# Making the low part of a weight split with an accumulating transfer in the down projection

## The chip, the cores and the metric

The kernel runs on one core of a Trainium2 chip. The metric is device time in microseconds (us) of one execution; lower is better. Before the change the median of three runs is 1138.18 us (1138.13 to 1138.3).

## The reference

One layer of a bidirectional encoder trunk over 1024 positions of width 1024, in float32: a combined input projection, three groups (convolution, recurrent, gating), an output projection, a gated feed-forward block, and a gate with an input embedding. The part that is changed belongs to the feed-forward block, whose inner width is 2816:

```python
h = rmsnorm(x, norm_ffn[l])
f = dwconv(h @ w_up[l], ffn_conv_w[l], ffn_conv_b[l], FFN_CONV_K // 2, FFN_CONV_K // 2)
fg, fu = jnp.split(f, 2, axis=-1)
x = x + (jax.nn.gelu(fg) * fu) @ w_down[l]
...
gate = jax.nn.sigmoid(rmsnorm(x, norm_ple[l]) @ w_ple_gate[l] + b_ple_gate[l])
```

## The kernel before, in words

TensorE multiplies in a reduced float32 format (fp32r). To keep accuracy, each operand is split into a high part, the value rounded to fp32r, and a low part, what the rounding lost. A product is then three matmuls that add into one accumulator: high by high, high by low, low by high (`mm3`). `split` makes the two parts: ScalarE copies the source into the high part with rounding, and VectorE subtracts the high part from the source to give the low part.

The down projection multiplies the gated activations g (2816 x 1024, kept transposed in DRAM as 22 tiles `g_dram[k]` of 128 x 1024) by w_down (22 row tiles of 128 x 1024). `prep_down` brings in one k: it loads `g_dram[k]` into a landing buffer (`raw`, three buffers that all such loads of the kernel share in turn), splits it, and calls `prep_rows`, which does the same for the row tile of w_down. Both loads are issued by SP. `down` runs one pass over up to four k: for each of the eight 128-row tiles of the output and each half of 512 columns, it adds 4 x 3 matmuls into an accumulator. The first pass (k = 0 to 3) is copied out by ScalarE; in later passes VectorE adds the accumulator to the running sum `x1` (tiles xA and xB). Passes 1 to 4 take k = 4 to 7, 8 to 11, 12 to 15 and 16 to 19; a last pass takes k = 20 and 21 and is joined with the gate. In pass 3 the residual rows are loaded and added too (`add_x1`).

A pass needs 16 buffers: high and low of g and of w for four k. There are two sets. Passes 0, 2 and 4 use the set `s1` (tiles L4, Y0, X3, L8, W0, L7, S0, W1 and the quarters of hT0 and hT1); passes 1 and 3 use `s2` (quarters of hT2, L0 to L3, quarters of hT3, G0 to G3). So in passes 1 and 3 the fourth tile of a pass stands in the tiles G, and in passes 2 and 4 the third and fourth stand in hT. A set can be filled again when the pass that used it has been multiplied, that is, while the other set is in use.

The order is not written by hand. Every operation is first recorded, and a planner (`Order`) then builds one order for all engines: it ranks the operations backwards from their users (`rank`, which puts a load 14 us, the constant FETCH, ahead of its user), places them one by one by estimated costs and landing times (`schedule`), plays that order through with shared transfers (`replay`), and keeps the best of six rounds by its own estimate (`plan`). The instructions are then issued in that order (line 461 issues them all, and so it is the line that every row of the profile names). Each engine takes its instructions in this fixed order and waits where an operand is not there. Transfers issued by GpSimd are in use for the constants at the start, the weights of the recurrent gates, eight stores of `e` and one load.

Of the kernel before, what the change touches and what calls it, by code (L numbers as in the profile page):

```python
# [10 lines left out]
F32 = mybir.dt.float32  # L11
F32R = mybir.dt.float32r
AF = mybir.ActivationFunctionType
ALU = mybir.AluOpType

P = 128
# [456 lines left out]
def encoder_layer(ctx, tc, x, p, norm_mix, w_in, conv_dw_w, conv_dw_b, conv_gn_g, conv_gn_b,  # L473
# [6 lines left out]
    V, A, PE, G, S = (Eng(od, e) for e in "VAPGS")  # L480
    x, p, out = x[0], p[0, 0], out[0]
    w_in, w_out, w_up, w_down = w_in[0], w_out[0], w_up[0], w_down[0]
# [20 lines left out]
    def raw(shape):  # L503
        return blk("raw", shape, bufs=3)
# [16 lines left out]
    def split(hi, lo, src, gain=None):  # L521
        if gain is None:
            A.activation(out=hi, in_=src, func=AF.Copy)
            V.tensor_tensor(out=lo, in0=src, in1=hi.bitcast(F32), op=ALU.subtract)
        else:
            A.activation(out=hi, in_=src, func=AF.Copy, scale=gain)
            V.scalar_tensor_tensor(out=lo, in0=src, scalar=gain, in1=hi.bitcast(F32),
                                   op0=ALU.mult, op1=ALU.subtract)
# [124 lines left out]
            r.append((hi, lo))  # L653
        return r

    def prep_rows(w, k, ring, gain=None):

        a = raw([P, T])
        S.dma_start(out=a, in_=w[k * P:(k + 1) * P, :])
        hi, lo = ring([P, T]), ring([P, T])  # L660
        split(hi, lo, a, gain)
        return hi, lo

    def mtile(wt, m, hT, ps=None, parts=((0, 512), (512, 512))):
# [87 lines left out]
    gl = [None] * 4  # L752
# [114 lines left out]
    e_dram = [od.tile(drp, [P, D], F32, f"e{t}", f"e{t}") for t in range(NT)]  # L867
    wple_r = Mixed("W4", "W5", "G2", "G3")
    wple = [prep_rows(w_ple, k, wple_r) for k in range(2)]
    ering = Ring(["L6", "L7", "L8"])  # L870
    rE = sm[:, 8:16]
# [162 lines left out]
    def w_out_rows(ring, *ks):  # L1034
        return [prep_rows(w_out, k, ring, cO[:, k:k + 1]) for k in ks]
# [194 lines left out]
    def set_of(*tags):  # L1230
        r = []
        for tag in tags:
            r += quarters(blk(tag, [P, 4, T], F32R)) if tag[0] == "h" else [tag]
        return r
# [3 lines left out]
    def prep_down(k, ring):  # L1238
        a = raw([P, T])
        S.dma_start(out=a, in_=g_dram[k])  # L1240
        gh, gl = ring([P, T]), ring([P, T])
        split(gh, gl, a)
        return (gh, gl), prep_rows(w_down, k, ring)

    def down(gw, after=None, first=False):
        n = len(gw)
# [22 lines left out]
    k = 0  # L1269
    sa = ["L4", "Y0", "X3", "L8", "W0", "L7", "S0", "W1"]  # L1270
    s1, s2 = sa + ["hT0", "hT1"], ["hT2"] + LS + ["hT3"] + GS
    for n, tags in enumerate((s1, s2, s1, s2, s1)):
        ring = Ring(set_of(*tags))
        down([prep_down(4 * n + j, ring) for j in range(4)], add_x1 if n == 3 else None, n == 0)
    k = 20
    ring = Ring(["L5", "L6"] + [f"W{j}" for j in range(2, 8)])
    last = [prep_down(k + j, ring) for j in range(2)]


# [3 lines left out]
    for k in range(8):  # L1283
        if k < 4:
            a = raw([P, T])
# [109 lines left out]
```

## Time and profile before

| | us |
|---|---|
| Median of three runs | 1138.18 |
| The profiled execution | 1138.66 |
| Its span, first to last instruction | 1136.9 |
| TensorE busy in the span | 1109.4 |
| VectorE busy | 820.5 |
| ScalarE busy | 558.5 |
| GpSimd busy | 25.5 |

The page gives the share of busy time of each engine and, in 40 slices, when it was busy. The table by stretch shows the same for chosen pieces of the span, with the granted TensorE clock and the load of the DMA engines. The timeline gives the instructions in order of start, with the idle time before one and what ended it. Pass 0 of the down projection begins at about 790 us among the last products of the up projection, pass 1 at about 836 us, pass 2 at about 880 us; one row tile of pass 3 runs from about 902 to 908 us, the rest from about 928 us; pass 4 begins at 967.5 us, and the gate follows.

### The profile page before, as it was taken

How to read it: one execution, taken by the hardware profiler on the slowest of the kernel's cores; microseconds unless marked ns; L12 is line 12 of the kernel's file. 1: busy time of each engine (PE TensorE's matmuls, PEld its weight loads, DVE VectorE, ACT ScalarE, POOL GpSimd, SP SyncE). 2: the span in 40 equal slices, each digit the busy share in tenths (PEclk: the TensorE clock that was granted, in tenths of full speed). 3: DMA queues.
4: the chain of work that ended last, by engine and by line, in shares of the span. 5: the costliest groups of instructions: out<-in, count | busy, mean ns of one | idle time of the engine just before them, and what ended most of it. 6: DMA issues, size and time to landing. Idle time of an engine off the chain costs nothing.

```text
span 1136.9 us, 13205 instructions
## 1 busy us (share of the span) xinstructions
PE 1109.4 (98%) x5305; PEld 929.8 (82%) x5305; DVE 820.5 (72%) x976; ACT 558.5 (49%) x720; POOL 25.5 (2%) x50
## 2 busy tenths in 40 slices
PE   6999999998999999999999999999999999999996
PEld 5987799887888888888888888888788888888885
DVE  6699999977966887687768776949433546654565
ACT  7555864779435475454545454536440222324445
POOL 3100100100000000000000000000000000000000
PEclk9999999999999999999999999999999999999999
DMA  8301240135032122232223222315640426421121
GB/s 296 99 1 56 94 162 20 53 101 185 22 122 96 39 74 93 75 111 74 69 80 112 74 74 75 111 56 192 235 147 2 148 85 212 130 75 40 72 74 55
DMA packets 55629, 110.60 MB, mean 97 GB/s; under 512 B 3977, under 2 KB 36594, under 8 KB 55568
## 3 DMA queue, kind: packets, MB, share of 16 engines
q1 hardware_dynamic: 53280, 104.35, 27.2%
q0 software_dynamic: 2288, 5.41, 1.3%
q8 instruction: 41, 0.67, 0.3%
q14 instruction: 20, 0.16, 0.0%
HBM read 85.63 MB, written 24.12 MB: 97 GB/s over the span
## 4 chain that ended last, share of the span: by engine, by line
PE 82%; DVE 13%; ACT 2%; issue 1%; DMA 1%; SPq 0%; DVEq 0%
PE pm L461 62%; PE pt L461 20%; DVE W L461 6%; DVE L L461 3%; DVE xA L461 1%; DMA xA<-in_x_dram 1%; DVE xB L461 1%; DVE G L461 1%; DVE hT L461 1%; ACT W L461 1%; ACT hT L461 0%; DMA raw<-in_w_down_dram 0%; ACT L L461 0%; ACT L461 0%; DVE V L461 0%
## 5 line engine op out<-in xcount | busy, mean ns | idle before, releaser
L461 PE MATMUL pm<-hT,W 128*128 128x512 f32 (+1 forms) x860 | 194.5, 369 | 0.1
L461 PEld LDWEIGHTS pm<-hT,W 128*128 128x128 f32 x860 | 149.8, 190 | 26.8 <-DVE hT L461 0.4
L461 PE MATMUL pm<-hT 128*128 128x512 f32 x480 | 124.6, 389 | 0.0
L461 PEld LDWEIGHTS pm<-hT 128*128 128x128 f32 x480 | 90.0, 188 | 19.2 <-DVE xA L461 0.4
L461 PE MATMUL pt<-hT,W 128*128 128x512 f32 x336 | 86.1, 389 | 0.0
L461 ACT ACTIVATE W<-raw 128x512 fp32r<-128x512 f32 (+1 forms) x60 | 44.9, 760 | 64.1 <-PE pt L461 47.8
L461 PEld LDWEIGHTS pt<-hT,W 128*128 128x128 f32 x336 | 63.1, 188 | 13.1
L461 DVE TENSOR_TENSOR xB<-xB,pm 128x512 f32<-128x512 f32 (+1 forms) x40 | 37.9, 950 | 42.5 <-PE pm L461 42.2
L461 PE MATMUL pm<-hT,hT 128*128 128x512 f32 (+1 forms) x256 | 66.2, 388 | 0.0
L461 ACT ACT_TABLE_LOAD x47 | 60.3, 1283 | 4.8 <-DVE W L461 2.4
L461 DVE TENSOR_TENSOR W<-raw,W 128x512 fp32r<-128x512 f32 (+1 forms) x57 | 47.1, 835 | 18.6 <-ACT W L461 18.6
L461 PEld LDWEIGHTS pm<-hT,hT 128*128 128x128 f32 x256 | 46.6, 188 | 8.9
L461 PE MATMUL pm<-L,L 128*128 128x512 f32 x160 | 50.3, 389 | 0.0
L461 DVE TENSOR_TENSOR xA<-xA,pm 128x1024 f32<-128x1024 f32 x20 | 24.4, 1219 | 35.1 <-PE pm L461 35.1
L461 DVE TENSOR_TENSOR X<-X,pm 128x512 f32<-128x512 f32 x20 | 13.7, 684 | 49.0 <-PE pm L461 49.0
L461 ACT ACTIVATE L<-raw 128x512 fp32r<-128x512 f32 (+1 forms) x19 | 15.8, 830 | 63.5 <-PE pm L461 35.0
L461 PE MATMUL pm<-xA,W 128*128 128x512 f32 x168 | 45.2, 389 | 0.0
L461 PE MATMUL pm<-W,hT 128*128 128x512 f32 x192 | 44.3, 390 | 0.0
L461 PE MATMUL pm<-L,hT 128*128 128x512 f32 (+1 forms) x160 | 43.7, 386 | 0.0
L461 ACT ACTIVATE hT<-raw 128x1024 fp32r<-128x1024 f32 x20 | 20.8, 1058 | 44.1 <-PE pm L461 31.4
L461 PEld LDWEIGHTS pm<-W,hT 128*128 128x128 f32 x192 | 35.9, 188 | 7.4
L461 PE MATMUL pt<-L,W 128*128 128x512 f32 x164 | 41.7, 390 | 0.0
(343 smaller groups left out, 2403.5 us busy)
## 6 DMA issues: line engine op xcount, KB each, us to landing
raw<-in_w_up_dram SPq DMA_DIRECT2D x44, 512.0 KB, 3.6
g<-xB SPq DMA_DIRECT2D x22, 512.0 KB, 2.7
raw<-g SPq DMA_DIRECT2D x22, 512.0 KB, 4.3
raw<-in_w_down_dram SPq DMA_DIRECT2D x22, 512.0 KB, 4.0
raw<-in_w_in_dram SPq DMA_DIRECT2D x16, 512.0 KB, 4.7
xA<-in_x_dram SPq DMA_DIRECT2D x8, 512.0 KB, 6.9
xB<-in_x_dram SPq DMA_DIRECT2D x8, 512.0 KB, 8.9
e<-L POOLq DMA_DIRECT2D x8, 512.0 KB, 3.2
```

The lines of the kernel that those rows point to most:

```text
L461: getattr(self.e[op.eng], meth)(*args, **kw)
```

## The change

`prep_rows` gets a flag `add`. With it, ScalarE writes the high part as before and then the negated high part into the low part's buffer; a transfer issued by GpSimd then reads the same rows of the weight from DRAM again and adds them to what stands in that buffer, which leaves weight minus high part. VectorE has no part in it. `prep_down` sets the flag for w_down tiles k = 4 to 19, that is, for passes 1 to 4; the split of g, and the tiles 0 to 3, 20 and 21 stay as they were.

```diff
-    def prep_rows(w, k, ring, gain=None):
+    def prep_rows(w, k, ring, gain=None, add=False):
 
         a = raw([P, T])
         S.dma_start(out=a, in_=w[k * P:(k + 1) * P, :])
         hi, lo = ring([P, T]), ring([P, T])
-        split(hi, lo, a, gain)
+        if add:
+
+            A.activation(out=hi, in_=a, func=AF.Copy)
+            A.activation(out=lo, in_=hi.bitcast(F32), func=AF.Copy, scale=-1.0)
+            G.dma_start(out=lo, in_=w[k * P:(k + 1) * P, :], accum_op=ALU.add)
+        else:
+            split(hi, lo, a, gain)
         return hi, lo
...
-        return (gh, gl), prep_rows(w_down, k, ring)
+        return (gh, gl), prep_rows(w_down, k, ring, add=4 <= k < 20)
```

## Rows read from the trace of the kernel before

**Rows 1.** The page's first two parts: busy time of each engine (share of the span, count of instructions), and the granted TensorE clock in 40 slices of 28.4 us, in tenths of full speed (9 is 90% or more).

```profile
PE 1109.4 (98%) x5305; PEld 929.8 (82%) x5305; DVE 820.5 (72%) x976; ACT 558.5 (49%) x720; POOL 25.5 (2%) x50
...
PEclk9999999999999999999999999999999999999999
```

**Rows 2.** Busy time by stretch: TensorE (count), its weight loads, VectorE, ScalarE, GpSimd, then granted clock, mean share of the DMA engines and GB/s.

```profile
0.00:50.00 50.00, 38.67 (x276) 36.78 (x276) 31.80 (x59) 30.49 (x52) 14.32 (x31) 1.00 0.64 214
...
100.00:200.00 100.00, 97.76 (x630) 88.21 (x629) 99.63 (x147) 63.37 (x83) 7.28 (x13) 1.00 0.24 84
200.00:300.00 100.00, 96.54 (x455) 79.77 (x453) 86.94 (x91) 75.52 (x80) 3.90 (x6) 0.98 0.29 96
...
780.00:810.00 30.00, 29.68 (x130) 24.16 (x131) 28.30 (x26) 20.38 (x21) 0.00 (x0) 1.00 0.78 261
810.00:833.00 23.00, 23.00 (x102) 18.64 (x102) 0.06 (x1) 4.11 (x4) 0.00 (x0) 1.00 0.30 123
833.00:849.00 16.00, 16.00 (x71) 12.90 (x70) 10.21 (x9) 10.09 (x10) 0.00 (x0) 1.00 0.62 200
849.00:881.00 32.00, 32.00 (x143) 26.40 (x142) 8.95 (x9) 2.35 (x3) 0.00 (x0) 1.00 0.10 32
881.00:897.00 16.00, 16.00 (x72) 13.28 (x71) 11.49 (x10) 5.93 (x6) 0.00 (x0) 1.00 0.69 234
897.00:930.00 33.00, 33.00 (x147) 27.32 (x147) 9.99 (x9) 2.62 (x3) 0.00 (x0) 1.00 0.09 30
930.00:952.00 22.00, 22.00 (x99) 18.23 (x98) 17.62 (x16) 7.78 (x8) 0.00 (x0) 1.00 0.79 263
952.00:1000.00 48.00, 48.00 (x214) 39.75 (x213) 28.65 (x24) 11.12 (x10) 0.00 (x0) 1.00 0.39 121
1000.00:1106.00 106.00, 106.00 (x497) 88.34 (x496) 59.22 (x60) 45.48 (x62) 0.00 (x0) 1.00 0.20 70
1106.00:1137.00 31.00, 21.60 (x122) 18.73 (x120) 16.95 (x31) 16.84 (x32) 0.00 (x0) 0.93 0.13 51
```

**Rows 3.** Waits of TensorE from 700 us to the end: who waited for whom, us in total, times, longest.

```profile
PE pm L461 <- ACT xA L461: 0.3, 1, 0.3
```

**Rows 4.** Timeline (start us, length us): the last splits of each pass's fill on VectorE and ScalarE, and the first matmuls on the tiles of passes 1 to 4.

```profile
808.83 1.23 DVE L461 TENSOR_TENSOR G<-raw,G 128x1024 fp32r<-128x1024 f32 x1 [0.78 <-ACT G L461]
...
840.70 0.84 PE L461 MATMUL pm<-G,G 128*128 128x512 f32 x3
...
848.23 1.23 DVE L461 TENSOR_TENSOR hT<-raw,hT 128x1024 fp32r<-128x1024 f32 x1 [0.86 <-ACT hT L461]
...
881.85 1.52 PE L461 MATMUL pm<-hT 128*128 128x512 f32 x6
...
892.74 1.06 ACT L461 ACTIVATE G<-raw 128x1024 fp32r<-128x1024 f32 x1 [1.47 <-DMA raw<-in_w_down_dram]
...
892.71 2.35 DVE L461 TENSOR_TENSOR G<-raw,G 128x1024 fp32r<-128x1024 f32 x2
...
903.61 0.84 PE L461 MATMUL pm<-hT 128*128 128x512 f32 x3
904.29 0.84 PE L461 MATMUL pm<-G,G 128*128 128x512 f32 x3
...
927.38 1.06 ACT L461 ACTIVATE L<-raw 128x1024 fp32r<-128x1024 f32 x1 [33.58 <-PE pm L461]
928.35 1.04 ACT L461 ACTIVATE X<-raw 128x1024 fp32r<-128x1024 f32 x1
...
940.97 2.22 ACT L461 ACTIVATE hT<-raw 128x1024 fp32r<-128x1024 f32 x2 [3.19 <-DMA raw<-g]
...
944.35 1.22 DVE L461 TENSOR_TENSOR hT<-raw,hT 128x1024 fp32r<-128x1024 f32 x1
...
968.89 1.52 PE L461 MATMUL pm<-hT 128*128 128x512 f32 x6
```

**Rows 5.** Timeline of ScalarE and TensorE at the one wait of the stage: a copy of a weight tile, the emptying of pass 0's first accumulator, and the matmul behind it.

```profile
807.74 1.06 ACT L461 ACTIVATE G<-raw 128x1024 fp32r<-128x1024 f32 x1 [0.69 <-DMA raw<-in_w_down_dram]
808.71 1.01 ACT L461 ACTIVATE xA<-pm 128x1024 f32<-128x1024 f32 x1
...
809.76 0.50 PE L461 MATMUL pm<-X,L 128*128 128x512 f32 x1 [0.32 <-ACT xA L461]
```

**Rows 6.** Groups of instructions of one shape, ScalarE from 833 to 1010 us and VectorE from 808 to 950 us: count, busy us, mean ns of one, idle time before them and who ended it.

```profile
L461 ACT ACTIVATE hT<-raw 128x1024 fp32r<-128x1024 f32 x12 | 12.6, 1062 | 39.9 <-PE pm L461 30.5 <-DMA raw<-g 6.7 <-DMA raw<-in_w_down_dram 2.6
...
L461 DVE TENSOR_TENSOR hT<-raw,hT 128x1024 fp32r<-128x1024 f32 x12 | 14.5, 1221 | 5.1 <-ACT hT L461 5.1
```

**Rows 7.** Transfers: GpSimd's only instruction after 250 us in the timeline (start, length, idle before), then issues by tile with the issuing queue, count, KB each and median us from issue to landing, and the least, median and longest landing of the loads of w_down.

```profile
270.99 0.59 POOL L461 DMA_DIRECT2D V<-in_norm_ffn_dram  x1 [56.26 <-PE pm L461]
...
raw<-in_w_down_dram SPq DMA_DIRECT2D x22, 512.0 KB, 4.0
...
e<-L POOLq DMA_DIRECT2D x8, 512.0 KB, 3.2
...
V<-in_norm_ffn_dram POOLq DMA_DIRECT2D x1, 512.0 KB, 5.7
...
DMA to landing us min/median/max: 3.3/4.0/8.3
```

**Rows 8.** Waits of SP's queue from 775 to 1010 us: us in total, times, longest.

```profile
SPq L461 <- DVE hT L461: 65.9, 22, 31.1
```

## The prediction

> **What bounds the kernel now.** I read the page first: TensorE is busy for 98% of the span, VectorE for 72%, ScalarE for 49%, and the granted clock is at its upper level in all 40 slices [rows 1]. A share of the whole span hides the stages, so the second view is the table by stretch [rows 2]. From 780 us to 1106 us, where the down projection and the start of the gate run, TensorE is idle only between 780 and 810 us, for 30.00 - 29.68 = 0.32 us; the later stretches show every microsecond as busy. Since a busy TensorE need not be a TensorE at its peak, I also looked at the spacing: three matmuls of 512 columns take 0.68 us from start to start (903.61, 904.29), 0.227 us each [rows 4] at clock 1.00. What is idle over the whole run, 1136.9 - 1109.4 = 27.5 us, lies elsewhere: 11.3 us in the first 50 us, 2.2 + 3.5 us between 100 and 300 us, 9.4 us in the tail after 1106 us [rows 2]. Third, the waits of TensorE after 700 us: one, for a ScalarE copy of an accumulated row, 0.3 us [rows 3]. So in the stage that is changed VectorE, ScalarE and the queues are all beside the path, and the question is only whether each tile is ready before the matmul that reads it.
>
> Each pass of the projection holds 8 x 2 x 4 x 3 = 192 matmuls, 192 x 0.227 = 43.6 us, and the 16 buffers of a pass are filled while the pass before it runs. The fourth reading is therefore, for each pass, the end of its last subtraction against the first matmul that needs that tile [rows 4]:
> - pass 1 (k = 4 to 7): 808.83 + 1.23 = 810.06 against 840.70, room of 30.6 us;
> - pass 2: 848.23 + 1.23 = 849.46 against about 882 (the two triples of matmuls on hT at 881.85), 32 us;
> - pass 3: 892.71 + 2.35 = 895.06 against 904.29, 9.2 us, since the planner puts the first row tile of pass 3 in the middle of pass 2;
> - pass 4: 944.35 + 1.22 = 945.57 against about 969 (968.89), 23 us.
>
> The tightest place, pass 3, decides the rival below.
>
> **The change, part by part.**
> Removed: 16 subtractions on VectorE of 1.22 us each [rows 6], 16 x 1.22 = 19.5 us. None is on the path: TensorE never waited for one after 700 us [rows 3]. Worth 0 to 0.32 us, the whole idle time of the stage; I take 0. Where the relief is largest, at 780 to 810 us (VectorE 28.30 of 30 us busy [rows 2]), TensorE's one wait was for ScalarE.
>
> Added on ScalarE: 16 negated copies. The same shape takes 1.06 us, and in a row they start 0.97 us apart (927.38, 928.35) [rows 4, 6], so 16 x 0.97 = 15.5 us. The copy waits only for the one before it on its own engine and for the buffer that the subtraction used to need, so nothing new blocks ScalarE's queue; what stands behind it is at most 0.97 us later. In passes 2 to 4 ScalarE has 8 to 10 us of work in a 16 to 22 us burst and under 3 us in the 32 us after it [rows 2], and the accumulated rows are taken off by VectorE there: cost 0. In 780 to 810 us it has 20.38 of 30 us, and it empties the accumulators too; there the four copies can stand in front of one of these. The shown case is 0.32 us, when the copy at 807.74 came before the emptying at 808.71 [rows 3, 5]. Bounds: 0 to 4 x 0.97 = 3.9 us; I take 0, nearest to that row, as the planner knows the copy's cost and ranks tiles of the next pass behind.
>
> Moved in time: the weights' landing buffer is now released by the copy and not by the subtraction after it, about 1.2 us earlier; SP's loads did wait for those subtractions, 65.9 us in 22 waits [rows 8]. The fill is not on the path, so this is 0 too, but it helps the new chain.
>
> Added on GpSimd's queue: 16 transfers of 512 KB that add in place. Issuing costs GpSimd about 0.59 us for a tile of this size [rows 7], and it had no instruction after 271 us; behind a waiting transfer stand only the transfers of later tiles. The trace shows no accumulating transfer, so its time A from issue to landing is bounded by neighbours [rows 7]: 3.2 us for a GpSimd-issued store of 512 KB below; above, twice the slowest load of w_down, 2 x 8.3 = 16.6 us, since the destination must be read as well. I take 5.7 us, the one GpSimd-issued load into such a tile, and one more passage of 0.524 MB at the 234 GB/s of 881 to 897 us [rows 2], 2.2 us: A = 7.9 us. It ends nearest to the 5.7 us row, which has engine, size and direction in common with it.
>
> The Trainium skill has a rule that speaks against the change (Collectives: The Full Stack, The bandwidth ceiling: the fold count and why AG ≠ RS ≠ AR): an addition in the DMA engines runs at half the rate of a copy, because two sources are read. No row here shows it. With the fixed 2.0 us and 436 GB/s that DMA: Bandwidth & Descriptors gives (Anatomy of one DMA), the plain transfer is 3.2 us, which the store's 3.2 us [rows 7] agrees with, and with doubled reading an estimate for A of 4.4 us; by the pages the sum would stay as it is.
>
> Engine capacity: the pass's eight loads keep the DMA engines 0.69 busy over 16 us [rows 2]; 234 / 0.69 = 339 GB/s is the full rate, 1.55 us for one passage. Eight loads and four additions of three passages are (8 + 12) x 1.55 = 31 us of a 43.6 us pass: it fits, and an addition's 4.6 us is about the 3 to 5 us between the weight copies of one pass, so they hardly pile up.
>
> The chain to the tightest tile: the copy of k = 15 ends at 892.74 + 1.06 = 893.80 [rows 4], the negated copy at 894.8, the addition at 894.8 + 7.9 = 902.7. The first use is at 904.29: in time by 1.6 us, if the order of TensorE stays. In pass 4 the last copy ends at 940.97 + 2.22 = 943.19, so A may reach 968.89 - 944.2 = 24 us there, and more in passes 1 and 2. So nothing reaches the path, and the sum is 0.
>
> Sum: the profiled execution took 1138.66 us, 1136.9 us of it span; 1138.66 + 0 = 1138.7, and the median of the runs is 0.48 us below that execution: **1138.2 us**.
>
> **The rivals.**
> *The addition comes late in pass 3 (slower).* TensorE's order is fixed when the kernel is built, so when one operand is late it stands. If the early row tile of pass 3 keeps its place, the stall is A - 9.5 us (904.29 - 894.8): it decides from A = 9.5 us on, is measurable from 11.8 us, and at A = 16.6 us costs 7.1 us: 1145.3 us. For it: the room of 9.2 us, no measured price, additions and loads at the same time. Against it: the planner charges the transfer with a landing time of its own before it places that row tile, and all other passes have much room. Should A exceed 24 us, more passes would be late and the time past 1150 us; nothing in the rows is that slow.
>
> *ScalarE in front of the emptying (slower).* The four copies at 780 to 810 us delay accumulators: up to 3.9 us, 1142 us. For it: the 0.3 us wait is of just this kind. Against it: 9.6 us of ScalarE are free in that stretch.
>
> *The order of everything is redrawn.* The planner builds the order from all operations at once, ranks each backwards from its users, and keeps the best of six rounds. The additions rank the weight loads about 13 us earlier than before (FETCH 14 and a copy in place of a subtraction), and another round may win. That can change the idle time outside the stage, 17 us in the first 300 us and 9.4 us in the tail, either way. A tenth of these 26.4 us gone would be 1138.2 - 2.7 = 1135.5 us; as much lost, 1140.9 us. For it: that idle time is real. Against it: the work of the first 700 us and of the tail is unchanged, and nothing in the change touches what those waits are for.
>
> *The change does nothing because the subtractions were hidden anyway*: this is the forecast itself.
>
> **How the numbers follow.** A measurement of this kernel tells about 0.2% from no change, 2.3 us: 1135.9 to 1140.5. Forecast, within that: 0.61. Late additions: 0.17. ScalarE in front: 0.06. Redrawn order: 0.12 faster, 0.04 slower. So faster 0.12, same 0.61, slower 0.27. The forecast's own range, with 0.32 us less and the small part of a stall, is 1137 to 1140. The range reaches down to 1135.5 (redrawn) and up to 1146 (A at its upper bound); I leave out about 0.16: larger redraws below, and additions slower than any row above.
>
> **What would show it.** Right: TensorE busy without a gap from 810 to 1106 us as in [rows 2]; 19.5 us less on VectorE and about 15.5 us more on ScalarE; additions landing in 5 to 10 us; in every pass the landing before the first matmul of its tile. The late rival: a wait of TensorE or of its weight load for the addition, at the first matmuls on G and L of a pass. ScalarE in front: waits for xA or xB at 800 to 815 us. Redrawn: the first 300 us or the tail with other idle time, and stage boundaries shifted already ahead of 760 us. I would be wrong if an addition took over 11.8 us, or if the new order left less room than the old.

## The result and the profile after

The changed kernel takes 1146.65 us, median of five runs (1144.17 to 1150.18), against 1138.18 us (1137.95 to 1139.7); the ratio is 1.0074, 95% interval 1.0055 to 1.0092. It is slower by more than the 0.2% that can be told, and 0.65 us above the stated range. The profiled execution after is the fastest of the five, 1144.17 us with a span of 1142.4 us; what the median has above it, 2.5 us, stands in no trace.

First the page and the table by stretch of the changed kernel, in the columns of [rows 1, 2]:

```profile
PE 1107.0 (97%) x5305; PEld 927.8 (81%) x5305; DVE 802.8 (70%) x961; ACT 567.9 (50%) x732; POOL 39.1 (3%) x66
```

```profile
0.00:50.00 50.00, 32.72 (x244) 31.43 (x245) 33.80 (x70) 30.28 (x54) 14.36 (x31) 1.00 0.61 204
50.00:100.00 50.00, 49.27 (x225) 40.32 (x224) 43.34 (x63) 39.15 (x37) 2.85 (x5) 1.00 0.11 35
100.00:200.00 100.00, 96.82 (x591) 85.95 (x590) 99.90 (x148) 45.61 (x63) 4.32 (x8) 1.00 0.24 82
...
810.00:833.00 23.00, 23.00 (x102) 18.82 (x102) 2.45 (x2) 9.90 (x10) 1.73 (x2) 1.00 0.94 289
...
897.00:930.00 33.00, 32.17 (x142) 26.32 (x141) 8.47 (x7) 2.64 (x3) 1.74 (x2) 1.00 0.44 124
...
1106.00:1142.00 36.00, 27.11 (x147) 23.30 (x145) 19.88 (x33) 17.89 (x33) 0.00 (x0) 0.93 0.15 59
```

Read the column of TensorE against [rows 2]. The first 50 us have 32.72 us of work where there were 38.67: most of the loss is 750 us ahead of the changed code. The stage that was changed has lost only 0.83 us, in 897 to 930 us. The work moved roughly as planned: VectorE 820.5 - 802.8 = 17.7 us less, ScalarE 9.4 us more (16 copies more, but three table loads fewer, among others), GpSimd 13.6 us more.

The waits of TensorE say who was late (us in total, times, longest); the first two lines are of the first 320 us, the other two of 780 us to the end:

```profile
PE pt L461 <- DVE L L461: 11.5, 3, 7.9
PE pt L461 <- DVE hT L461: 7.0, 3, 6.0
...
PE pm L461 <- DMA G<-in_w_down_dram: 0.8, 1, 0.8
PE pm L461 <- DVE hT L461: 0.4, 1, 0.4
```

The early ones are waits for the normalised rows and their transposes at the very start of the kernel. The same two in the kernel before, in the same window:

```profile
PE pt L461 <- DVE L L461: 8.6, 3, 8.0
PE pt L461 <- DVE hT L461: 3.2, 1, 3.2
```

All waits of TensorE in these 320 us together are 16.7 us before and 24.4 us after. Of the four lines of the changed kernel, only the third is the change at work: the addition into G, the fourth tile of pass 3, the place that the prediction named. Here are the issue of this addition and the matmul that waited, in the timeline:

```profile
898.90 0.87 POOL L461 DMA_DIRECT2D G<-in_w_down_dram  x1 [0.97 <-ACT G L461]
...
909.07 0.73 PE L461 MATMUL pm<-G,G 128*128 128x512 f32 x2 [0.83 <-DMA G<-in_w_down_dram]
```

And the view of the DMA queues: GpSimd's queue (packets, MB, share of 16 engines' span), then the additions by tile as in [rows 7]:

```profile
q0 software_dynamic: 4592, 13.80, 5.3%
...
hT<-in_w_down_dram POOLq DMA_DIRECT2D x8, 512.0 KB, 8.5
L<-in_w_down_dram POOLq DMA_DIRECT2D x4, 512.0 KB, 7.9
G<-in_w_down_dram POOLq DMA_DIRECT2D x2, 512.0 KB, 7.8
W<-in_w_down_dram POOLq DMA_DIRECT2D x2, 512.0 KB, 8.1
```

These are medians by tile, 7.8 to 8.5 us from issue to landing; the estimate was 7.9 us. The single additions took 5.4 to 10.8 us, and the one that TensorE waits for, issued at 898.90 us, took 10.1 us.

The kernel's own planner explains why the start changed. It keeps the best of six rounds by its estimate; before, the first round was the best, with the change the fourth. The two programs do the same work at the start of the kernel, but the fourth round puts it in another order than the first.

### The profile page after: what moved, and what is told of

Same layout as the page of the kernel before. It is cut to its first block, busy times and chain, and to the rows that moved or that the text cites. A ratio compares the mean times of both kernels' runs of the same rounds, so it can differ in the third digit from the quotient of the medians.

```text
span 1142.4 us, 13234 instructions
## 1 busy us (share of the span) xinstructions
PE 1107.0 (97%) x5305; PEld 927.8 (81%) x5305; DVE 802.8 (70%) x961; ACT 567.9 (50%) x732; POOL 39.1 (3%) x66
## 5 line engine op out<-in xcount | busy, mean ns | idle before, releaser
L461 DVE TENSOR_TENSOR X<-X,pm 128x512 f32<-128x512 f32 x20 | 13.7, 683 | 67.0 <-PE pm L461 67.0
L461 ACT ACTIVATE xB<-xB 128x1024 f32<-128x1024 f32 x22 | 23.3, 1061 | 40.0 <-DVE xB L461 40.0
```

The source lines that it names most:

```text
L461: getattr(self.e[op.eng], meth)(*args, **kw)
```

## The experiments

Theory R: the loss is the redrawn order, above all the other round. Theory D: it is the additions themselves, late or in the way. A third, L, came out of the first runs. The runs were made in three rows (1 to 3, 4 to 7, 8 and 9); in each the kernel before ran on the same chip beside them, with a median of 1137.83, 1138.15 and 1138.27 us.

**1. The change, held to the planner's first round.** In `plan`, on the changed kernel:

```diff
-            if best is None or span < best[0]:
+            if n == 0:
```

> The change in full, but the planner is held to the order of its first round, the round that the kernel before was issued in; up to the output projection's second half (about 340 us) the order is then the kernel before's. Theory R (the loss comes from the redrawn order: with the change, the planner's own estimates make another of its six rounds win, and the new order has more idle TensorE time in the first 300 us): TensorE busy 38 to 39 us in the first 50 us, as before, and 1138 to 1140 us, what is left over 1138.2 being a late addition of about 1 us. Theory D (the additions and copies themselves cost the time, by late operands and contention in the down projection): 1144 to 1147 us, as the changed kernel.

Measured: 1149.08 us (1148.4 to 1149.93), ratio 1.0098 (1.0085 to 1.0112). The start is as before (38.88 us of TensorE in 50 us), and yet it is the slowest of all. R alone had failed. Timeline of ScalarE and TensorE in this run:

```profile
816.53 1.06 ACT L461 ACTIVATE G<-raw 128x1024 fp32r<-128x1024 f32 x1 [5.29 <-DMA raw<-in_w_down_dram]
817.62 1.06 ACT L461 ACTIVATE G<-G 128x1024 fp32r<-128x1024 f32 x1
818.58 1.01 ACT L461 ACTIVATE xA<-pm 128x1024 f32<-128x1024 f32 x1
...
819.64 0.70 PE L461 MATMUL pm<-X,L 128*128 128x512 f32 x1 [4.48 <-ACT xA L461]
820.13 0.63 PE L461 MATMUL pm<-L,L 128*128 128x512 f32 x1
820.56 0.63 PE L461 MATMUL pm<-X,Y 128*128 128x512 f32 x1
```

And the landing of all transfers from w_down, additions included, in the view of that tensor (least, median, longest), then the table by stretch:

```profile
DMA to landing us min/median/max: 3.4/7.6/13.9
...
810.00:833.00 23.00, 18.52 (x75) 14.73 (x74) 1.23 (x1) 6.57 (x7) 0.87 (x1) 0.93 0.70 206
```

ScalarE stands 5.29 us for the plain load of k = 7, which took 13.9 us from issue at 802.56 to landing; the slowest before took 8.3 us [rows 7]. Behind that copy, in ScalarE's fixed order, stand its negated copy (817.62) and the emptying of an accumulator, and TensorE waits 4.48 us for the latter. Then its matmuls start 0.43 us apart, not 0.227 us, for some 3 us: the granted clock of 810 to 833 us is 0.93 here, so part of that stretch ran at the lower level. Two more waits follow, 2.5 us for an emptied accumulator and 0.8 us for an addition. The 2.5 us stand behind a load too, on VectorE: its additions into xA come after a split that waits 10.68 us for ScalarE's copy of a g tile, which waits for loads. From 780 to 1006 us TensorE stands 226 - 218.24 = 7.8 us and starts 945 matmuls, where the kernel before stands 0.3 us and starts 992; 47 x 0.227 = 10.7 us, so of the loss about 3 us are matmuls at the lower clock. Theory L: an addition keeps the DMA engines so long that the plain loads beside it come late, and what stands behind these loads in the fixed orders comes late with them.

**2. The kernel before, held to the planner's fourth round.** The same edit with `if n == 3:` on the kernel before; no additions.

> The kernel before, without any addition, held to the order of the planner's fourth round, the one that the changed kernel was issued in; up to about 350 us the order is then the changed kernel's. Theory R: 1143 to 1147 us and TensorE busy near 33 us in the first 50 us, with the wide spread of the changed kernel's runs, though no addition is there. Theory D: 1138 us, as before.

Measured: 1145.48 us (1144.03 to 1145.62), ratio 1.0064 (1.005 to 1.0077). The table by stretch:

```profile
0.00:50.00 50.00, 32.57 (x243) 31.28 (x244) 33.64 (x70) 30.32 (x54) 14.35 (x31) 1.00 0.60 204
```

The waits of TensorE in the first 320 us:

```profile
PE pt L461 <- DVE L L461: 11.6, 3, 8.0
PE pt L461 <- DVE hT L461: 7.1, 3, 6.0
```

These are the waits of the changed kernel, without one addition. So the other round costs 1145.48 - 1137.83 = 7.6 us, as R expected. The wide spread did not come with it.

**3. The changed kernel, transfers that overwrite.** `accum_op=ALU.add` is taken out of the transfer; the order is the changed kernel's. The low part is then the weight itself, so the kernel leaves out the subtraction of the high part and its result is not the layer's.

> The changed kernel in its own order, instruction for instruction, but the 16 transfers of GpSimd overwrite and do not add, so that the low part of these weight tiles is the weight itself. Theory R: 1145 to 1147 us still; only the 0.8 us wait for the late addition goes, and the plain transfer lands in 4 to 6 us against 7.6 us. Theory D: 1139 to 1142 us, since the reading of the destination is gone.

Measured: 1145.57 us (1143.13 to 1145.81), ratio 1.0062 (1.0049 to 1.0075), as R expected: in the issued order of the changed kernel, adding costs about 1 us at most, and that is not clear of noise (1.0074, 1.0055 to 1.0092, with the adding). The landing is a little over the 4 to 6 us expected. The view of the DMA queues, to be set beside that of after:

```profile
q0 software_dynamic: 4592, 13.80, 3.5%
...
hT<-in_w_down_dram POOLq DMA_DIRECT2D x8, 512.0 KB, 6.9
L<-in_w_down_dram POOLq DMA_DIRECT2D x4, 512.0 KB, 5.6
G<-in_w_down_dram POOLq DMA_DIRECT2D x2, 512.0 KB, 6.0
W<-in_w_down_dram POOLq DMA_DIRECT2D x2, 512.0 KB, 5.5
```

Before, this queue took 1.3% of 1136.9 us on the page, 14.8 us of all 16 engines. Less that, 16 plain transfers took 0.035 x 1143.8 - 14.8 = 25.2 us, 1.58 us each, and 16 additions 0.053 x 1142.4 - 14.8 = 45.8 us, 2.86 us each: 1.8 times as long, for the same bytes counted. (The shares are rounded to 0.1%, so each sum is good to some 0.6 us.)

**4. Experiment 1, transfers that overwrite.** The edits of 1 and 3 together.

> The change held to the planner's first round, as in the run with 1149 us, instruction for instruction, but the 16 transfers overwrite and do not add, so that the low part of these tiles is the weight itself. That run's loss has one long wait for an accumulator (4.5 us) behind a load of w_down that took 13.9 us, and two shorter ones. Theory L (an addition keeps the DMA engines longer than a plain transfer, and the plain loads beside it come late): the waits shrink to under 1 us each, the slowest load of w_down is back near 8 to 10 us, and the time is 1138 to 1141 us. Theory B (it is the additional 8 MB in themselves, added or not): about 1146 to 1149 us.

Measured: 1137.7 us (1136.14 to 1138.89), ratio 0.9995 (0.9985 to 1.0005). All 11 us of experiment 1 are gone with the adding alone, at the same order and the same number of transfers: theory L, and not the 8 MB more in themselves. The waits of TensorE after 700 us in this run:

```profile
PE pm L461 <- DVE xA L461: 0.7, 1, 0.7
PE pm L461 <- ACT xA L461: 0.3, 1, 0.3
```

The landing of its transfers from w_down:

```profile
DMA to landing us min/median/max: 3.4/5.7/10.1
```

The slowest is the load of k = 7 again, issued at 802.77 us: 10.1 us here, 13.9 us in run 1, 5.4 us in the kernel before. So the further plain transfers, or the order that differs from before, delay it too; the 3.8 us that adding puts on top are what the order has no room for.

**5. The kernel before in its own order, with additions.** At issue, the place of each subtraction is taken by two instructions:

```diff
+        split(hi, lo, a, gain)
         if add:
...
+            od.swap[od.ops[-1]] = [
+                ("A", "activation", (), dict(out=lo, in_=hi.bitcast(F32), func=AF.Copy, scale=-1.0)),
+                ("G", "dma_start", (), dict(out=lo, in_=w[k * P:(k + 1) * P, :], accum_op=ALU.add))]
...
-            for meth, args, kw in op.calls:
+            for e, meth, args, kw in self.swap.get(op, [(op.eng, *c) for c in op.calls]):
```

> The kernel before in its own order to the last matmul; only at the place of each of the 16 subtractions stand the negated copy on ScalarE and the addition on GpSimd. This is the sum of the prediction, with the planner taken out of it. The prediction's theory (each addition lands ahead of its matmuls): 1138 to 1139 us, no wait over 0.5 us from 780 to 1000 us. Rival, late addition in pass 3: one wait of 0 to 2 us at the first G of pass 3 near 904 us, 1138 to 1141 us. Theory L (additions make the plain loads late, and ScalarE, which waits for such a load, has the emptying of an accumulator behind it): a wait of TensorE for ScalarE's xA or xB between 805 and 820 us of 3 to 6 us, and 1141 to 1146 us.

Measured: 1143.9 us (1141.66 to 1146.81), ratio 1.0057 (1.0038 to 1.0077). This is the sum of the prediction, and it is 5.7 us off. The time is in theory L's range; its one wait of 3 to 6 us came as two of 1.4 and 1.5 us, and the late addition came beside it. Timeline of TensorE (its four waits from 780 to 1000 us), then of ScalarE at three of them, and of ScalarE and GpSimd for the tightest tile:

```profile
808.59 0.50 PE L461 MATMUL pm<-X,L 128*128 128x512 f32 x1 [1.50 <-ACT xB L461]
812.28 0.50 PE L461 MATMUL pm<-X,L 128*128 128x512 f32 x1 [1.36 <-ACT xA L461]
840.55 0.96 PE L461 MATMUL pm<-hT 128*128 128x512 f32 x3 [0.60 <-ACT xB L461]
909.80 0.73 PE L461 MATMUL pm<-G,G 128*128 128x512 f32 x2 [2.04 <-DMA G<-in_w_down_dram]
...
804.36 1.06 ACT L461 ACTIVATE hT<-raw 128x1024 fp32r<-128x1024 f32 x1 [2.37 <-DMA raw<-in_w_down_dram]
...
806.59 1.04 ACT L461 ACTIVATE hT<-hT 128x1024 fp32r<-128x1024 f32 x1
807.53 1.00 ACT L461 ACTIVATE xB<-pm 128x1024 f32<-128x1024 f32 x1
810.26 1.06 ACT L461 ACTIVATE G<-raw 128x1024 fp32r<-128x1024 f32 x1 [1.72 <-DMA raw<-in_w_down_dram]
811.23 1.01 ACT L461 ACTIVATE xA<-pm 128x1024 f32<-128x1024 f32 x1
...
838.55 1.04 ACT L461 ACTIVATE L<-X 128x1024 fp32r<-128x1024 f32 x1
839.50 1.00 ACT L461 ACTIVATE xB<-pm 128x1024 f32<-128x1024 f32 x1
...
894.15 1.06 ACT L461 ACTIVATE hT<-raw 128x1024 fp32r<-128x1024 f32 x1 [3.09 <-DMA raw<-in_w_down_dram]
899.53 1.06 ACT L461 ACTIVATE G<-raw 128x1024 fp32r<-128x1024 f32 x1 [1.36 <-DMA raw<-in_w_down_dram]
...
901.98 0.88 POOL L461 DMA_DIRECT2D G<-in_w_down_dram  x1 [4.32 <-ACT G L461]
```

1.50 + 1.36 + 0.60 + 2.04 = 5.5 us, nearly the whole loss. Both rivals of the prediction are here at their places. Of ScalarE's share, the 1.36 us stand behind a late load (810.26), the 0.60 us behind a negated copy (838.55), and the 1.50 us behind one of each (804.36, 806.59). The load of 810.26 is that of k = 7: it was issued at 802.33 us, as before (802.34), and took 7.9 us where it took 5.4. The addition for k = 15 was reckoned to be issued at 894.8 us and was issued at 901.98: the copies for k = 14 and 15 start at 894.15 and 899.53, where the last one started at 892.74 [rows 4]. Of these 7.2 us, 3.5 us are no loss of room, since the three waits ahead of it shift the first use as well, from 904.29 to 909.80 - 2.04 = 907.76. The other 3.7 us leave 5.8 us of room for a landing that took 7.8 us. They come from the loads: that of k = 14 took 8.2 us (4.5 before), and that of k = 15 was issued at 895.24 (889.19 before), after a wait of SP for the copy of k = 14. This order was not run with overwriting transfers, so how its loss divides between the adding and the further transfers is not shown here.

**6. Experiment 1 without pass 1's additions.** `add=8 <= k < 20`, first round.

> First round of the planner, and only the tiles k = 8 to 19 with the addition; those of pass 1 are split as before. Theory L: pass 1's tiles are filled beside the last loads of the stage before, where the DMA engines are busiest and ScalarE empties accumulators; without the additions there, the wait of 4.5 us near 815 us and the slower clock behind it go, some 6 us: 1140 to 1143 us, with the waits near 860 and 905 us still there. If the loss had another place: 1147 us or more.

Measured: 1144.68 us (1144.14 to 1145.19), ratio 1.0063 (1.0048 to 1.0078). Half a hit: from 780 to 897 us TensorE is now busy throughout, which fits a stall near 815 us that comes from pass 1's additions. It does not prove it, since the planner, given other ranks, drew the order anew. The only wait of TensorE after 700 us is that for G in pass 3, 2.3 us. But the time is above the forecast, with time lost elsewhere in the new order (the waits, then the table by stretch, same columns):

```profile
PE pm L461 <- DMA G<-in_w_down_dram: 2.3, 1, 2.3
...
300.00:400.00 100.00, 96.77 (x452) 79.99 (x451) 70.97 (x74) 41.54 (x76) 0.00 (x0) 0.97 0.23 79
```

**7. Experiment 1, with the planner told what an addition costs.** Three times the bytes and 3.0 for 0.9 us of landing, in `schedule` (and the bytes in `replay`):

```diff
+                nb *= 3 if "accum_op" in op.calls[0][2] else 1
...
-                end = dma + 0.9 if op.land is None else max(dma + 0.9, t + op.land)
+                end = dma + (3.0 if "accum_op" in op.calls[0][2] else 0.9) if op.land is None else max(dma + 0.9, t + op.land)
```

> The change in full in the planner's first round, but the planner is told that an addition moves three times its bytes and lands 2.1 us later than it assumed. Theory L: if the stalls are an order built on too short a landing time, the planner now puts the accumulators' emptying and the early matmuls elsewhere, and the time falls from 1149 us to 1138 to 1143 us. If it stays at 1147 us or more, the engines' time for additions is the limit, whatever the order.

Measured: 1136.61 us (1135.19 to 1137.63), ratio 0.9986 (0.9977 to 0.9995), better than forecast. All 16 additions are there; the stalls are not. The waits of TensorE after 700 us:

```profile
PE pm L463 <- ACT xA L463: 0.4, 1, 0.4
```

The slowest plain load still took 13.7 us. So the engines can carry the additions, and late loads need not cost anything; it was the order that could not carry them. With these costs the planner also takes the first round by its own choice, and the issued order is this one.

**8. and 9. That order with subtractions, and experiment 7 again.** In 8, at issue, the negated copy's place is taken by VectorE's subtraction and the transfer is left out:

```diff
+            od.swap[od.ops[-1]] = [("V", "tensor_tensor", (),
+                                    dict(out=lo, in0=a, in1=hi.bitcast(F32), op=ALU.subtract))]
             G.dma_start(out=lo, in_=w[k * P:(k + 1) * P, :], accum_op=ALU.add)
+            od.swap[od.ops[-1]] = []
```

> The order of the run with 1136.6 us (first round, planner told what an addition costs), instruction for instruction, but at the place of each negated copy VectorE subtracts as before, and the 16 transfers of GpSimd are left out. If what that run has over the kernel before comes from its order: 1136 to 1137 us again. If it comes from the work taken off VectorE and the landing buffers freed earlier: 1138 us or more.

> The run with 1136.6 us once more, beside the one above on the same chip, to tell the two apart: 1136 to 1137.5 us, 0.05 to 0.25% under the kernel before.

Measured: 1136.48 us (ratio 0.9983, 0.9974 to 0.9992) with subtractions, 1136.41 us (0.9982, 0.9974 to 0.9991) with additions. The 0.2% over the kernel before are the order's; between adding and subtracting there is nothing to be told. Table by stretch of run 9, then of run 8:

```profile
780.00:810.00 30.00, 30.00 (x134) 24.75 (x133) 22.05 (x21) 23.52 (x24) 2.67 (x3) 1.00 0.84 262
...
881.00:897.00 16.00, 16.00 (x72) 13.25 (x71) 7.29 (x7) 8.27 (x8) 3.37 (x4) 1.00 1.00 275
```

```profile
780.00:810.00 30.00, 30.00 (x133) 24.34 (x132) 26.72 (x25) 20.49 (x21) 0.00 (x0) 1.00 0.77 252
...
881.00:897.00 16.00, 16.00 (x72) 13.28 (x71) 12.15 (x11) 5.32 (x5) 0.00 (x0) 1.00 0.72 223
```

TensorE is full in both; VectorE has 12.15 us of work in 16 with subtractions and 7.29 us with additions, and it makes no difference.

## Why the prediction was wrong

**What bounds the kernel** was right, and with it that the subtractions are worth nothing: runs 8 and 9 differ by 0.07 us. In the order of these two the sum of 0 holds.

**The step that failed most: the redrawn order.** It was a rival, with a price of 2.7 us either way and a chance of 0.04 for slower, on the argument that "the work of the first 700 us and of the tail is unchanged". The work is unchanged, but the order is chosen as a whole, and another of the six rounds has another start. The price was a tenth of the idle time, taken without a reason for that share. Run 2 gives the price, 7.6 us, and the waits at the start show its place. This is most of the measured 8.5 us (1146.65 - 1138.18).

**The second: "the sum is 0".** In the order of before the additions cost 5.7 us (run 5), in the re-ranked first round 11.3 us (run 1: 1149.08 - 1137.83), in the order that was issued about 1 us at most (run 3 against the result). The duration A was right as a median, 7.9 us estimated, 7.8 to 8.5 measured; at the tightest place of the changed kernel it was 10.1 us. What failed above all is the start of the chain: the landing of the plain loads was carried over from [rows 4] as if the additions did not touch it. The capacity sum (31 of 43.6 us) even had an addition too dear, 4.6 us of the engines for the 2.86 of run 3. But it is an average over a pass, and loads and additions come in one burst: [rows 2] showed 0.62 to 0.79 busy there before anything was added, and it is up to 0.94 after. Three landing buffers then hand a late load on to the next, as for k = 14 and 15 in run 5.

The Trainium skill's rule that an addition in the DMA engines runs at half the rate of a copy (Collectives: The Full Stack, The bandwidth ceiling: the fold count and why AG ≠ RS ≠ AR) is stated there for the add of a ring collective, which no run here has; run 3 beside after comes near it, 2.86 against 1.58 us of the engines, 1.8 times. The prediction's estimate of 4.4 us for the landing, by the 2.0 us and 436 GB/s of the Trainium skill (DMA: Bandwidth & Descriptors, Anatomy of one DMA), was too short: the quickest addition took 5.4 us. The 3.2 us that the same figures give for a plain transfer agreed with the store of [rows 7], but not with the load of 5.7 us beside it.

**"Nothing new blocks ScalarE's queue"** was wrong in its scope. The negated copy indeed adds no wait beyond its own length, but the copy of the high part ahead of it waits for a load, and that load was now late; in runs 1 and 5 the accumulators stood behind it. The rival ScalarE in front of the emptying had the right place (808 to 820 us) and the smaller half of the cause: run 5 shows 0.60 us and a part of 1.50 us from the copies themselves, the rest from waiting for a transfer. Of run 1's 4.48 us, the negated copy between load and emptying (817.62 to 818.58) is 0.96 us and the late load the rest.

**Late addition in pass 3**: right in place, 0.83 us in the changed kernel, 2.04 us in run 5. In the changed kernel the mechanism is the rival's too: the room from issue to first use was 909.07 - 0.83 - 898.90 = 9.3 us, and the landing took 10.1. In run 5 the landing was as estimated, 7.8 us, and the room had shrunk to 5.8 us by the late loads.

**The tail** kept its idle time, 36.00 - 27.11 = 8.9 us to 1142 us, 9.4 us before [rows 2]. **Open**: the spread of the changed kernel's five runs, 6 us, which neither run 2 (1.6 us) nor run 3 (2.7 us) showed and run 5 did (5.2 us); in runs 7 and 9, which add without a stall, it is 2.4 us. Open is also why run 8's order is 0.2% better than that of before. A part can be seen, 0.5 us less idle between 300 and 400 us and 0.3 us at 780 to 810 us; the rest was not followed up.

## What to carry to other kernels

Where an automatic planner orders the whole program, test a local edit with the order held, as in runs 2, 5 and 8: otherwise the draw of the order (7.6 us here) can hide what the edit does. Where a transfer becomes heavier, ask which loads share its burst and what stands behind the engine that waits for those loads; its own landing time is the smaller part of the question. And when an operation of a new kind enters a planned order, give the planner its cost: that alone turned 1149 us into 1136.6 us, though the cost given was only near the measured one (three times the bytes, where 1.8 times the engines' time was measured).

## What the runs showed of the hardware

An adding transfer of 512 KB took 2.86 us of all 16 DMA engines, an overwriting one of the same shape 1.58 us. It landed in 7.8 to 8.5 us against 5.5 to 6.9 us (medians by tile; single ones 5.4 to 10.8 us against 4.1 to 8.6 us), and GpSimd was busy 0.87 us with its issue, 0.54 us without the adding. The slowest plain load of w_down took 8.3 us before, 10.1 us (run 4) and 11.9 us (run 3) beside overwriting transfers, and 13.9 us (run 1) and 16.5 us (run 5) beside additions. After a stall of TensorE of 4.5 us its matmuls started 0.43 us apart for some 3 us, where 0.227 us is the rule, with a granted clock of 0.93 in that stretch (run 1): a late operand cost more than its wait.
